# The lead of a gated residual block: how x and c arrive, three unsplit contracted chunks, and half 1's square sum on VectorE

## The chip, the cores and the metric

The kernel runs on one core of a Trainium2 chip. The metric is the device time of one execution in microseconds (us). Five engines share the work: TensorE (PE, with PEld for its weight loads), VectorE (DVE), ScalarE (ACT), GpSimd (POOL) and SyncE (SP), which only issues DMAs.

## The reference

One layer of a streaming encoder, with 1024 positions, 1024 channels and a feed-forward width of 2816, all in fp32:

```
mod = silu(c) @ w_ada + b_ada;  sh1, sc1, g1, sh2, sc2, g2 = split(mod, 6)
h = rms_norm(x, norm_mix_g) * (1 + sc1) + sh1
b, c_s, v, v_c, gl, gates = split(h @ w_in)                  # 7 blocks of 1024 columns
y_a = (b * causal_dwconv3(c_s * v)) @ w_short_out
u = causal_dwconv31(v_c * sigmoid(gl)) + conv_conf_b
y_b = silu(layer_norm(u)) @ w_conf_out
x = x + g1 * ((sigmoid(g_a) * y_a + sigmoid(g_b) * y_b) @ w_o)
h2 = rms_norm(x, norm_ffn_g) * (1 + sc2) + sh2
a, bg = split(h2 @ w_ffn_in);  x = x + g2 * ((silu(a) * bg) @ w_ffn_out)
out = rms_norm(x, final_norm_g)
```

Here `rms_norm` divides by the root of the mean square over the 1024 channels. The host transposes, reorders and packs the inputs.

## The kernel before, in words

Channels lie on partitions: x is held transposed, as eight chunks (k = 0 to 7) of 128 channels by 1024 positions. Positions come in two halves of 512 (h = 0 and 1), as a PSUM bank holds 512 fp32 numbers a partition. A tile of 128x512 is the unit of most steps.

A large matrix product is made of *split* operands. Each operand is cut into a high part in fp32r (a ScalarE copy, `wh` for weights) and a low part, the rest (a subtraction, `wl`). `mm3` (L274) makes a product of three matmuls: high by high (L277), weight high by activation low (L278) and weight low by activation high (L280). The norm sums (`ss` at L393, later `mu` and `var`) are single matmuls of unsplit fp32 operands with a matrix of ones, which also spreads the sum over all partitions.

The **lead** is the first stage. It makes seven blocks of 128 output columns of the input projection (three pairs for the GLU, one gate), contracted over all eight chunks, first for half 0, then for half 1. `row_blocks` (L358) runs chunk by chunk: for each k it makes the operands and then feeds seven accumulating banks; the last two chunks are done together, bank by bank. The operands of chunk k come out of `act_x` (L430):

- two blocks of `w_ada` are loaded and reduced with silu(c) on VectorE (`modulation`, L254, one instruction of 128x1024 at L262 and a short one that reads the sum out). They give scale and shift of the chunk; `affine` (L267) joins the scale to the norm's gain.
- `modulate` (L342) multiplies x by the scale column and the reciprocal root r in one VectorE instruction (L344), ScalarE adds the shift into the high part `h..h` (L346), VectorE makes the low part `h..l` (L347), and ScalarE writes the whole, unsplit h back over x (L350), for sums that later products need.
- `lead_w` (L427) loads and splits the chunk's 128x896 weights: the high part on ScalarE (L203), the low part on VectorE, or on GpSimd for chunks 5 to 7 (L204).

Ahead of that, `squares_x` (L377) loads half 0's x as eight tiles of 128x512, whose rows are 2 KB, squares them on ScalarE (L383) and adds them on VectorE (L388). `norm_start` (L391) sums over partitions on TensorE and starts the reciprocal root on ScalarE (L327), `rstd_end` finishes it in three VectorE steps (L332 to L334). c is loaded spread over 128 partitions (512 KB, L422) and put through Silu in one 128x1024 instruction (L424); the vectors `vec` follow on the same queue (L423). Half 1's x is loaded and squared after chunk 2 (`X1_AT = 2`), and its squares are added on GpSimd (L388); its norm sum and root stand among chunks 4 and 5.

The order is written by hand in places: `tc.issue_after` puts an instruction behind another one on its engine, and `plan` with `next_w` fetches weights two blocks ahead. Nearly all loads go through SP's queue in program order, and one of them waits there, with all behind it, until its buffer is free. Buffers bear on this: `raw` has five (loaded weights), `wh` and `wl` have three each, `uc` has eight (ada blocks in the lead, later the GLU's results and more), PSUM has six banks for `ps` and two for `ps2`.

Behind the lead come one block of gate b, the remaining input columns in pairs (`product`, a seven-product scheme in place of eight block products), the convolutions on VectorE, the two output projections, the joined one and the feed-forward part.

Of the kernel before, what the change touches and what calls it, by code (L numbers as in the profile page):

```python
# [47 lines left out]
CK = 31  # L48
# [12 lines left out]
ADA_ORDER = [b for k in range(KC) for b in (8 + k, k)] + list(range(16, 48))  # L61


LEAD = 7


X1_AT = 2


AHEAD = 2  # L70
# [28 lines left out]
PIECES = [(0, 512), (512, 256), (768, 256)]  # L99


FILL = 264


@with_exitstack
def block_kernel(ctx: ExitStack, tc: tile.TileContext, xT, c, vecs, ada, w_first, w_plain, w_duals,
                 w_short, w_conf, w_o, w_fi, w_fo, w_last, outT):
# [14 lines left out]
    cp = pool("const", 1)  # L122
# [53 lines left out]
    def modc(i):  # L176
        return mod[:, i : i + 1]
# [16 lines left out]
    def weights(src, n=1024, after=(), lo_engine=nc.vector):  # L194
        return split_w(load(src, n), n, after, lo_engine)
# [37 lines left out]
        return {m: (lambda m=m: unit(m)) for m in PRODUCTS}  # L233


    plan = [(w_first[k], LEAD * P) for k in range(KC)]
    plan += [(w_plain[0], 1024)]
    for d in range(len(PAIRS) // 2):
        units = dual_units([w_duals[d, m] for m in range(4)], 1024, eng=nc.gpsimd)
# [5 lines left out]
    def next_w(ahead=AHEAD):  # L245

        fetch(ahead + 1)
        return ready.pop(0)
# [23 lines left out]

    def mm3(outs, wsl, w, xs, first, last, again=False):

        wh, wl = w[0][:, wsl], w[1][:, wsl]
        for ps, (xh, xl) in zip(outs, xs):
            nc.tensor.matmul(ps, wh, xh, start=first, stop=False, skip_group_check=again)  # L277
            nc.tensor.matmul(ps, wh, xl, start=False, stop=False, skip_group_check=again)  # L278
        for ps, (xh, _) in zip(outs, xs):
            mm3.ins = nc.tensor.matmul(ps, wl, xh, start=False, stop=last, skip_group_check=again).ins  # L280
# [61 lines left out]
    def modulate(src, r, scale, shift, name):  # L342

        begin = nc.vector.scalar_tensor_tensor(out=src, in0=src, scalar=scale, in1=r, op0=ALU.mult, op1=ALU.mult)  # L344
        hi, lo = hl_tile(name + "h"), hl_tile(name + "l")
        act = nc.scalar.activation(hi, src, AF.Identity, bias=shift)  # L346
        last = nc.vector.scalar_tensor_tensor(  # L347
            out=lo, in0=src, scalar=shift, in1=f32(hi), op0=ALU.add, op1=ALU.subtract
        )
# [5 lines left out]

        return [(next_w(), act(k)) for k in range(n)]

    def row_blocks(act, n, name, ops=(), unit=lambda k: next_w()):  # L358

        outs = [(ps_tile if o < 6 else ps2_tile)(f"{name}{o}") for o in range(n)]  # L360
        ops = list(ops)
        for k in range(KC):
            if k == len(ops):
                xs = act(k)
                ops.append((unit(k), xs))
            if k == KC - 2:
                continue
            for o in range(n):
                for kk in range(KC - 2, KC) if k == KC - 1 else (k,):
                    w, xs = ops[kk]  # L370
                    mm3([outs[o]], slice(o * P, o * P + P), w, [xs], kk == 0, kk == KC - 1)
        return outs


    x = {}

    def squares_x(h):  # L377

        for k in range(KC):
            x[k, h] = s_tile(f"x{k}{h}")  # L380
            nc.sync.dma_start(x[k, h], xT[k, :, halves[h]])
            sq = g_tile("sq")
            nc.scalar.activation(sq, x[k, h], AF.Square, scale=1.0 / 32.0)  # L383
            if k == 0:
                acc = sq
            else:
                eng = nc.gpsimd if h else nc.vector
                eng.tensor_tensor(acc, acc, sq, ALU.add)  # L388
        return acc

    def norm_start(acc, name, n=H, tile_of=g_tile, ss_tile=ps_tile):  # L391
        ss = ss_tile("ss")
        nc.tensor.matmul(ss[:, :n], ones, acc, start=True, stop=True)  # L393
        return rstd_start(ss, eps1, name, n, tile_of)
# [5 lines left out]
    def uc_tile(name, n=T + CK - 1, dt=F32):  # L400
        return ucp.tile([P, T + CK - 1], dt, tag="uc", name=name)[:, :n]
# [16 lines left out]
        nc.scalar.dma_start(gate_dram[b, j][:, halves[h]], sig)  # L418

    hT = [[None, None] for _ in range(KC)]  # L420
    rx_0 = rstd_end(*norm_start(squares_x(0), "rx0"))
    nc.sync.dma_start(cs, c.to_broadcast([P, D]))  # L422
    nc.sync.dma_start(vec, vecs)  # L423
    silu = nc.scalar.activation(cs, cs, AF.Silu)  # L424
    load_rsqrt(silu.ins)

    def lead_w(k):  # L427
        return weights(w_first[k], LEAD * P, modulate.ins[:1], nc.gpsimd if k > X1_AT + 2 else nc.vector)

    def act_x(k, h):  # L430
        nonlocal rx_1
        if h == 0:
            with ExitStack() as after:
                if k:
                    after.enter_context(tc.issue_after(modulate.ins[0]))
# [3 lines left out]
        hT[k][h] = modulate(x[k, h], rx_1 if h else rx_0, aff1[:, k : k + 1], modc(k), f"h{k}{h}")  # L439
        if h == 0:  # L440
            if k == X1_AT:
                rx_1 = squares_x(1)
            elif k == X1_AT + 2:
                with tc.issue_after(mm3.ins), tc.issue_after(modulate.ins[1]):
                    rx_1 = norm_start(rx_1, "rx1", ss_tile=ps2_tile)
            elif k == X1_AT + 3:
                with tc.issue_after(modulate.ins[2]):
                    rx_1 = rstd_end(*rx_1)
        return hT[k][h]

    rx_1 = None
    for h in range(2):
        lead = row_blocks(lambda k: act_x(k, h), LEAD, "lead", **({} if h else {"unit": lead_w}))
        for j in range(LEAD // 2):
            glu(j, h, lead[2 * j], lead[2 * j + 1])
        gate("b", 0, h, lead[-1])
# [124 lines left out]


    taps = vec[:, V_CW : V_CW + CK // 2 * 2 * KC].rearrange("p (j two k) -> p j two k", two=2, k=KC)
    nc.vector.tensor_tensor(wsum.rearrange("p (j k) -> p j k", k=KC), taps[:, :, 0], taps[:, :, 1], ALU.add)
# [369 lines left out]
    n = 2 * GROUP * P  # L954
# [77 lines left out]
    for i in range(len(PIECES)):  # L1032
        acc, sqs = sqs[0] if i else None, []
# [85 lines left out]
```

## Time and profile before

| | us |
|---|---|
| median of 3 runs | 1529.91 (1529.85 to 1535.77) |
| the profiled execution | 1529.94 |
| its span, first to last instruction | 1528.0 |
| TensorE busy | 1468.8 (96%) |
| VectorE busy | 1183.9 (77%) |
| ScalarE busy | 616.9 (40%) |
| GpSimd busy | 597.2 (39%) |
| mean granted TensorE clock | 0.989 |
| first lead matmul; first of half 1 | 20.34; 73.02 |

A matmul's duration in the profile includes its way through the array, so that following ones overlap; the cost in a stream is the distance of their starts. An unsplit fp32 matmul shows as two records. A group's idle time is that of its engine just before it, with the engine or DMA that ended it. The execution took 1.9 us more than its span; that lies around the program.

### The profile page before, as it was taken

The page shows a single profiled execution, that of the slowest core. Times are in us where ns is not written, and L with a number is a line of the kernel's source. Part 1 is how long each engine was busy: PE and PEld are TensorE (multiplying, and loading weights), DVE is VectorE, ACT ScalarE, POOL GpSimd, SP SyncE. Part 2 cuts the span into 40 slices and gives each one's busy share as a digit, 9 for nine tenths or more (in the row PEclk, how much of TensorE's full clock was granted, in tenths as well). Part 3 has the DMA queues.
Part 4 walks back from the last instruction along what each step waited for, and adds up shares of the span by engine and source line. Part 5 has one row for each costly group of instructions (what it writes and reads, how often), then busy time and mean ns, then how long its engine had stood idle before and what let it go on. Part 6 is the DMA issues. An engine that isn't in the chain of part 4 may idle for free.

```text
span 1528.0 us, 17853 instructions
## 1 busy us (share of the span) xinstructions
PE 1468.8 (96%) x6466; PEld 1205.1 (79%) x6466; DVE 1183.9 (77%) x1559; ACT 616.9 (40%) x873; POOL 597.2 (39%) x493
## 2 busy tenths in 40 slices
PE   5799999999998999999999989999999999999996
PEld 3688887877886888878788868888888888888886
DVE  7987898999998882757876798877766765677756
ACT  5563433333333343325334464444444443221234
POOL 1326788798768884310121101110000016535005
PEclk9999999999999999999999999999999999999998
DMA  9432214223222249755665527644444449999403
GB/s 363 161 101 69 97 56 152 69 97 111 97 69 97 70 171 393 262 182 178 236 203 158 173 83 234 207 152 155 153 153 152 154 150 367 351 304 274 129 15 111
DMA packets 88024, 256.16 MB, mean 168 GB/s; under 512 B 10112, under 2 KB 12288, under 8 KB 87936
## 3 DMA queue, kind: packets, MB, share of 16 engines
q1 hardware_dynamic: 47248, 147.01, 29.0%
q0 software_dynamic: 36944, 95.44, 19.2%
q10 hardware_dynamic: 3744, 12.58, 2.0%
q8 instruction: 50, 0.82, 0.2%
q14 instruction: 38, 0.31, 0.1%
HBM read 188.41 MB, written 66.58 MB: 167 GB/s over the span
## 4 chain that ended last, share of the span: by engine, by line
PE 67%; DVE 15%; DMA 6%; POOL 5%; issue 5%; ACT 1%; SPq 0%; DVEq 0%; ACTq 0%; POOLq 0%
PE x L280 10%; PE x L278 9%; PE x L277 9%; DVE c L604 6%; PE z L278 5%; PE z L280 5%; PE z L277 5%; PE y L277 3%; PE y L278 3%; PE y L280 3%; POOL wl L204 3%; DMA raw<-in_ada 2%; PE mix L277 2%; PE mix L278 2%; PE mix L280 2%
## 5 line engine op out<-in xcount | busy, mean ns | idle before, releaser
L203 ACT CAST wh<-raw 128x1024 fp32r<-128x1024 f32 (+2 forms) x260 | 262.0, 1009 | 406.1 <-PE z L278 100.6
L204 POOL TENSOR_TENSOR wl<-raw,wh 128x1024 fp32r<-128x1024 f32 (+1 forms) x95 | 243.1, 2564 | 96.3 <-ACT wh L203 89.8
L204 DVE TENSOR_TENSOR wl<-raw,wh 128x1024 fp32r<-128x1024 f32 (+2 forms) x165 | 190.2, 1155 | 50.4 <-ACT wh L203 47.8
L604 DVE SCALAR_TENSOR_TENSOR c<-diff,vec,c 128x512 f32<-128x512 f32 x248 | 182.5, 750 | 3.7
L867 POOL DMA_DIRECT2D hid<-stage x71 | 37.8, 533 | 356.2 <-DVE stage L317 350.8
L277 PE MATMUL x<-th,wh 128*128 128x512 f32 x336 | 130.7, 389 | 0.0
L278 PE MATMUL x<-tl,wh 128*128 128x512 f32 x336 | 130.7, 389 | 0.0
L280 PE MATMUL x<-th,wl 128*128 128x512 f32 x336 | 130.7, 389 | 0.0
L604 DVE SCALAR_TENSOR_TENSOR c<-u,wsum,c 128x512 f32<-128x512 f32 x112 | 84.2, 752 | 2.0
L277 PE MATMUL x<-t2h,wh 128*128 128x512 f32 x184 | 73.8, 403 | 5.5 <-ACT wh L203 2.8
L280 PE MATMUL x<-t2h,wl 128*128 128x512 f32 x184 | 73.5, 400 | 5.2 <-POOL wl L204 4.9
L278 PE MATMUL x<-t2l,wh 128*128 128x512 f32 x184 | 73.6, 400 | 0.1
L262 DVE CUSTOM_DVE_ANT_0 raw<-raw,cs,vec 128x1024 f32<-128x1024 f32 x24 | 33.7, 1405 | 51.6 <-DMA raw<-in_ada 47.6
L278 PEld LDWEIGHTS x<-tl,wh 128*128 128x128 f32 x336 | 63.1, 188 | 13.2
L280 PEld LDWEIGHTS x<-th,wl 128*128 128x128 f32 x336 | 63.1, 188 | 13.1
L277 PEld LDWEIGHTS x<-th,wh 128*128 128x128 f32 x336 | 63.1, 188 | 13.0
L280 PE MATMUL z<-th,wl 128*128 128x512 f32 x168 | 65.5, 390 | 0.0
L277 PE MATMUL z<-th,wh 128*128 128x512 f32 x168 | 65.4, 389 | 0.0
L278 PE MATMUL z<-tl,wh 128*128 128x512 f32 x168 | 65.4, 389 | 0.0
L316 ACT CAST stage<-g 128x512 fp32r<-128x512 f32 x62 | 38.3, 620 | 52.0 <-DVE g L856 24.7
L893 POOL DMA_DIRECT2D th<-hid x71 | 37.9, 534 | 52.0 <-PE x L280 31.8
L317 DVE TENSOR_TENSOR stage<-g,stage 128x512 fp32r<-128x512 f32 x62 | 42.5, 688 | 17.2 <-ACT stage L316 16.9
(811 smaller groups left out, 4091.0 us busy)
## 6 DMA issues: line engine op xcount, KB each, us to landing
hid<-stage POOLq DMA_DIRECT2D x71, 512.0 KB, 4.2
raw<-in_w_fi SPq DMA_DIRECT2D x50, 512.0 KB, 4.1
raw<-in_w_duals SPq DMA_DIRECT2D x48, 512.0 KB, 3.6
th<-hid POOLq DMA_DIRECT2D x71, 256.0 KB, 5.8
tl<-hid POOLq DMA_DIRECT2D x71, 256.0 KB, 5.9
ada<-in_ada SPq DMA_DIRECT2D x24, 512.0 KB, 7.7
raw<-in_ada SPq DMA_DIRECT2D x24, 512.0 KB, 4.7
raw<-in_w_fo SPq DMA_DIRECT2D x24, 384.0 KB, 5.9
```

The costliest lines, as they stand in the source:

```text
L203: nc.scalar.copy(wh, raw)
L204: lo = lo_engine.tensor_tensor(wl, raw, f32(wh), ALU.subtract)
L262: nc.vector.tensor_tensor_reduce(out=raw, in0=raw, in1=cs, scale=1.0, scalar=col(V_ADA, b), op0=ALU.mult, op1=ALU.add, accum_out=modc(b),)
L277: nc.tensor.matmul(ps, wh, xh, start=first, stop=False, skip_group_check=again)
L278: nc.tensor.matmul(ps, wh, xl, start=False, stop=False, skip_group_check=again)
L280: mm3.ins = nc.tensor.matmul(ps, wl, xh, start=False, stop=last, skip_group_check=again).ins
L316: nc.scalar.copy(hi, src)
L317: nc.vector.tensor_tensor(lo, src, f32(hi), ALU.subtract)
L604: tap.ins = nc.vector.scalar_tensor_tensor(out=out, in0=src[:, s : s + H], scalar=wt, in1=acc, op0=ALU.mult, op1=ALU.add).ins
L867: nc.gpsimd.dma_start(hid_dram[key], s)
L893: nc.gpsimd.dma_start(t, hid_dram[key][:, s])
```

## The change

It rebuilds the lead; all behind it keeps its code, but for `wsum`, a small sum of convolution weights, which moves behind a modulate.

- Half 0's x comes from a second array `x0`, in which two chunks lie side by side: four loads of 128x1024 with rows of 4 KB. They take four of the eight `uc` buffers; `modulate` reads them and writes into a new tile.
- c is loaded as one row on ScalarE's queue, and so is `vec`. Two fp32 matmuls with a row of ones spread c over the partitions in PSUM, where Silu reads it in two instructions of 128x512, behind the squares. A one-column Silu at the start loads its table.
- For half 0's chunks 0 to 2 (`WHOLE = 3`) neither weights nor h are split: `mm3` makes one fp32 matmul of the loaded weights and the whole h. Their h is split in half 1, and all weights are loaded again there, as before.
- Half 0's last two chunks are no longer joined (`joined=1`). All low parts of weights in the lead are made on VectorE.
- Half 1's x is loaded after chunk 5 (`X1_AT = 5`), squared and added on VectorE in chunk 6, its norm sum stands in chunk 6, the root's end behind chunk 7. Half 1's first operands are made ahead of half 0's GLUs.
- `FILL`, a tile that only shifts addresses, grows by 32 bytes a partition, and there is one more small constant tile.

```diff
+WHOLE = 3
-X1_AT = 2
+X1_AT = 5
-FILL = 264
+FILL = 272
...
     def mm3(outs, wsl, w, xs, first, last, again=False):
+        if w[1] is None:
+            for ps, x in zip(outs, xs):
+                mm3.ins = nc.tensor.matmul(ps, w[0][:, wsl], x, start=first, stop=last).ins
+            return
...
-    def modulate(src, r, scale, shift, name):
-        begin = nc.vector.scalar_tensor_tensor(out=src, in0=src, scalar=scale, in1=r, op0=ALU.mult, op1=ALU.mult)
+    def modulate(src, r, scale, shift, name, begun=None):
+        begin = nc.vector.scalar_tensor_tensor(
+            out=src, in0=src if begun is None else begun, scalar=scale, in1=r, op0=ALU.mult, op1=ALU.mult
+        )
+        if name is None:
+            act = nc.scalar.activation(src, src, AF.Identity, bias=shift)
+            modulate.ins = begin.ins, act.ins, begin.ins
+            return None
...
-    def squares_x(h):
-        for k in range(KC):
-            x[k, h] = s_tile(f"x{k}{h}")
-            nc.sync.dma_start(x[k, h], xT[k, :, halves[h]])
+    def squares_x(src, acc=None):
+        for t in src:
             sq = g_tile("sq")
...
-                eng = nc.gpsimd if h else nc.vector
-                eng.tensor_tensor(acc, acc, sq, ALU.add)
+                add = nc.vector.tensor_tensor(acc, acc, sq, ALU.add)
...
-    rx_0 = rstd_end(*norm_start(squares_x(0), "rx0"))
-    nc.sync.dma_start(cs, c.to_broadcast([P, D]))
-    nc.sync.dma_start(vec, vecs)
-    silu = nc.scalar.activation(cs, cs, AF.Silu)
+    crow = diffp.tile([P, T + CK - 1], F32, tag="diff", name="diff")[:1, :D]
+    nc.scalar.dma_start(crow, c)
+    nc.scalar.dma_start(vec, vecs)
+    nc.scalar.activation(cp.tile([P, 1], F32, name="si"), ones[:, :1], AF.Silu)
+    xin = {}
+    for k in range(0, KC, 2):
+        t = uc_tile("x0", T)
+        nc.sync.dma_start(t, x0[k // 2])
+        xin[k], xin[k + 1] = (t[:, s] for s in halves)
+    cb = []
+    for s in halves:
+        cb.append(ps_tile("cb"))
+        nc.tensor.matmul(cb[-1], ones[:1], crow[:, s], start=True, stop=True)
+    acc = squares_x([xin[k] for k in range(KC)])
+    with tc.issue_after(squares_x.ins[0]):
+        for s, t in zip(halves, cb):
+            silu = nc.scalar.activation(cs[:, s], t, AF.Silu)
     load_rsqrt(silu.ins)
+    rx_0 = rstd_end(*norm_start(acc, "rx0"))
     def lead_w(k):
-        return weights(w_first[k], LEAD * P, modulate.ins[:1], nc.gpsimd if k > X1_AT + 2 else nc.vector)
+        if k < WHOLE:
+            return load(w_first[k], LEAD * P), None
+        return weights(w_first[k], LEAD * P, modulate.ins[:1])
...
             if k == X1_AT:
-                rx_1 = squares_x(1)
-            elif k == X1_AT + 2:
+                for i in range(KC):
+                    x[i, 1] = s_tile(f"x{i}1")
+                    nc.sync.dma_start(x[i, 1], xT[i, :, halves[1]])
+            elif k == X1_AT + 1:
+                with tc.issue_after(modulate.ins[2]):
+                    rx_1 = squares_x([x[i, 1] for i in range(KC)])
                 with tc.issue_after(mm3.ins), tc.issue_after(modulate.ins[1]):
                     rx_1 = norm_start(rx_1, "rx1", ss_tile=ps2_tile)
-            elif k == X1_AT + 3:
+            elif k == KC - 1:
                 with tc.issue_after(modulate.ins[2]):
                     rx_1 = rstd_end(*rx_1)
+            if whole:
+                return x[k, 0]
+        elif k < WHOLE:
+            hT[k][0] = split(x[k, 0], hl_tile, f"h{k}0")
         return hT[k][h]
...
+    ops = ()
     for h in range(2):
-        lead = row_blocks(lambda k: act_x(k, h), LEAD, "lead", **({} if h else {"unit": lead_w}))
+        lead = row_blocks(lambda k: act_x(k, h), LEAD, "lead", ops, **({} if h else {"unit": lead_w, "joined": 1}))
+        if h == 0:
+            xs = act_x(0, 1)
+            ops = [(next_w(), xs)]
...
+        "x0": x[:H].T.reshape(KC // 2, 2, P, H).transpose(0, 2, 1, 3).reshape(KC // 2, P, T),
```

More of the change, by code (lines that the diff above doesn't have):

```diff
@@ L99, with block_kernel @@
 PIECES = [(0, 512), (512, 256), (768, 256)]
-FILL = 264
+FILL = 272
 @with_exitstack
-def block_kernel(ctx: ExitStack, tc: tile.TileContext, xT, c, vecs, ada, w_first, w_plain, w_duals,
+def block_kernel(ctx: ExitStack, tc: tile.TileContext, x0, xT, c, vecs, ada, w_first, w_plain, w_duals,
                  w_short, w_conf, w_o, w_fi, w_fo, w_last, outT):
@@ L233, in dual_units @@
         return {m: (lambda m=m: unit(m)) for m in PRODUCTS}
-    plan = [(w_first[k], LEAD * P) for k in range(KC)]
+    plan = [None] * KC
     plan += [(w_plain[0], 1024)]
@@ L356, in first_operands, with row_blocks @@
         return [(next_w(), act(k)) for k in range(n)]
-    def row_blocks(act, n, name, ops=(), unit=lambda k: next_w()):
+    def row_blocks(act, n, name, ops=(), unit=lambda k: next_w(), joined=2):
         outs = [(ps_tile if o < 6 else ps2_tile)(f"{name}{o}") for o in range(n)]
@@ L365, in row_blocks @@
                 ops.append((unit(k), xs))
-            if k == KC - 2:
+            if KC - joined <= k < KC - 1:
                 continue
             for o in range(n):
-                for kk in range(KC - 2, KC) if k == KC - 1 else (k,):
+                for kk in range(KC - joined, KC) if k == KC - 1 else (k,):
                     w, xs = ops[kk]
@@ L375, in block_kernel @@
     x = {}
-    def squares_x(h):
-        for k in range(KC):
-            x[k, h] = s_tile(f"x{k}{h}")
-            nc.sync.dma_start(x[k, h], xT[k, :, halves[h]])
+    def squares_x(src, acc=None):
+        for t in src:
             sq = g_tile("sq")
-            nc.scalar.activation(sq, x[k, h], AF.Square, scale=1.0 / 32.0)
-            if k == 0:
+            act = nc.scalar.activation(sq, t, AF.Square, scale=1.0 / 32.0)
+            if acc is None:
                 acc = sq
             else:
-                eng = nc.gpsimd if h else nc.vector
-                eng.tensor_tensor(acc, acc, sq, ALU.add)
+                add = nc.vector.tensor_tensor(acc, acc, sq, ALU.add)
+        squares_x.ins = act.ins, add.ins
         return acc
@@ L433, in act_x @@
             with ExitStack() as after:
-                if k:
-                    after.enter_context(tc.issue_after(modulate.ins[0]))
+                after.enter_context(tc.issue_after(modulate.ins[0] if k else squares_x.ins[1]))
                 for i in range(2 * k, 2 * k + 2):
@@ L438, in act_x @@
             affine(aff1, k, 8, V_GMIX)
-        hT[k][h] = modulate(x[k, h], rx_1 if h else rx_0, aff1[:, k : k + 1], modc(k), f"h{k}{h}")
+            x[k, 0] = s_tile(f"x{k}0")
+        whole = h == 0 and k < WHOLE
+        hT[k][h] = modulate(x[k, h], rx_1 if h else rx_0, aff1[:, k : k + 1], modc(k),
+                            None if whole else f"h{k}{h}", None if h else xin[k])
         if h == 0:
             if k == X1_AT:
-                rx_1 = squares_x(1)
-            elif k == X1_AT + 2:
+                for i in range(KC):
[4 more added lines that the diff above has]
+                    rx_1 = squares_x([x[i, 1] for i in range(KC)])
                 with tc.issue_after(mm3.ins), tc.issue_after(modulate.ins[1]):
                     rx_1 = norm_start(rx_1, "rx1", ss_tile=ps2_tile)
-            elif k == X1_AT + 3:
+            elif k == KC - 1:
                 with tc.issue_after(modulate.ins[2]):
                     rx_1 = rstd_end(*rx_1)
+            if whole:
+                return x[k, 0]
+        elif k < WHOLE:
+            hT[k][0] = split(x[k, 0], hl_tile, f"h{k}0")
         return hT[k][h]
     rx_1 = None
+    plan[:KC] = [lambda k=k: weights(w_first[k], LEAD * P, [modulate.ins[2 if k else 0]]) for k in range(KC)]
+    ops = ()
     for h in range(2):
-        lead = row_blocks(lambda k: act_x(k, h), LEAD, "lead", **({} if h else {"unit": lead_w}))
+        lead = row_blocks(lambda k: act_x(k, h), LEAD, "lead", ops, **({} if h else {"unit": lead_w, "joined": 1}))
+        if h == 0:
+            xs = act_x(0, 1)
+            ops = [(next_w(), xs)]
         for j in range(LEAD // 2):
@@ L583, in block_kernel @@
     taps = vec[:, V_CW : V_CW + CK // 2 * 2 * KC].rearrange("p (j two k) -> p j two k", two=2, k=KC)
-    nc.vector.tensor_tensor(wsum.rearrange("p (j k) -> p j k", k=KC), taps[:, :, 0], taps[:, :, 1], ALU.add)
+    with tc.issue_after(modulate.ins[0]):
+        nc.vector.tensor_tensor(wsum.rearrange("p (j k) -> p j k", k=KC), taps[:, :, 0], taps[:, :, 1], ALU.add)
     cv_dram = [dram.tile([P, T], F32, name=f"cv{j}") for j in range(KC)]
```

## The prediction

> **What bounds the kernel now.** I first cut the span into stretches. Columns: stretch, its length, then busy time (and count) of PE, PEld, DVE, ACT and POOL, the granted clock, DMA share, GB/s.
>
> ```profile
> 0.00:75.00 75.00, 47.90 (x181) 36.28 (x182) 64.68 (x93) 40.36 (x57) 18.95 (x15) 0.95 0.72 265
> 75.00:125.00 50.00, 50.00 (x222) 41.40 (x222) 43.67 (x53) 30.00 (x46) 16.38 (x8) 1.00 0.27 80
> 125.00:600.00 475.00, 466.24 (x2039) 382.69 (x2038) 409.02 (x527) 179.66 (x244) 374.89 (x164) 1.00 0.33 114
> ```
>
> TensorE is idle for 27 of the first 75 us, never in the next 50 and for 9 of the 475 after that. The lead is the only place in the first 600 us with much to gain, and what it gains reaches the end: behind it TensorE is the bound. From the end of the lead on (a few instructions later on VectorE and ScalarE) the changed program issues the same instructions in the same order on every engine.
>
> Then TensorE's waits up to 75 us (total, count, longest) and its time line.
>
> ```profile
> PE ss L393 <- DVE sq L388: 12.2, 1, 12.2
> PE lead L277 <- ACT h00h L346: 6.0, 1, 6.0
> PE lead L278 <- DVE h30l L347: 4.7, 1, 4.7
> PE lead L277 <- ACT h60h L346: 1.9, 1, 1.9
> PE lead L277 <- ACT h70h L346: 1.4, 1, 1.4
> PE lead L277 <- ACT h30h L346: 0.8, 1, 0.8
> ```
> ```profile
> 20.34 1.22 PE L277 MATMUL lead<-h00h,wh 128*128 128x512 f32 x2 [6.02 <-ACT h00h L346]
> ...
> 43.45 0.80 PE L278 MATMUL lead<-h30l,wh 128*128 128x512 f32 x1 [4.69 <-DVE h30l L347]
> ...
> 73.02 0.39 PE L277 MATMUL lead<-h01h,wh 128*128 128x512 f32 x1
> ```
>
> Call the first lead product P0 (20.34 now) and the first product of half 1 T1 (73.02 now). Split products stand 0.227 us apart, so half 0's 168 and one norm sum (0.87, below) need 39 of those 52.7 us. The 13.7 lost are 8.8 of waits (4.7, 1.9, 1.4, 0.8) and about 5 of products 0.43 apart, behind 20.34 and again behind 43.45: half rate after TensorE stood still. The long wait is for h30l, and the time line of VectorE and GpSimd shows why it is late:
>
> ```profile
> 37.95 3.98 POOL L388 TENSOR_TENSOR sq<-sq 128x512 f32<-128x512 f32 x2 [0.30 <-ACT sq L383]
> ```
> ```profile
> 36.45 2.16 DVE L204 TENSOR_TENSOR wl<-raw,wh 128x896 fp32r<-128x896 f32 x1
> 38.53 2.29 DVE L262 CUSTOM_DVE_ANT_0 ada<-ada,cs,vec 128x1024 f32<-128x1024 f32 x1
> ```
>
> These two take 1.08 and 1.28 where GpSimd is idle. Half 1's adds on GpSimd slow VectorE, and half 1's x (2 MB) stands ahead of chunk 4's loads.
>
> **The change, part by part.**
>
> *Start.* Let L be when the last of half 0's x lands. It is 10.2 now: issued at 4.0, 6.2 to landing. The stretches of the queue:
>
> ```profile
> 2.00:8.00 6.00, 0.00 (x0) 0.00 (x0) 1.39 (x2) 2.26 (x5) 0.00 (x0) 1.00 0.96 289
> 8.00:10.00 2.00, 0.00 (x0) 0.00 (x0) 1.48 (x3) 1.85 (x4) 0.00 (x0) 1.00 1.02 352
> 10.00:20.00 10.00, 2.07 (x2) 0.50 (x2) 8.10 (x14) 6.73 (x9) 0.00 (x0) 1.00 1.02 408
> 27.00:33.00 6.00, 6.00 (x29) 4.95 (x28) 5.96 (x11) 4.18 (x7) 0.06 (x1) 1.00 1.06 392
> ```
>
> By 10.2 some 2.6 MB have moved, of which 2.1 are x and 0.5 belong to transfers still under way. After the change 0.19 MB of vec share the engines, issued by ScalarE; c is one row of 4 KB. So 2.8 MB must move. At the rates of now that is done at 10.9; at 408 GB/s, the rate of 4 KB rows from 10 us on, at 2.0 + 6.8 = 8.8. The profile does not tell whether 2 to 8 us are slow because of 2 KB rows or because the program has just started: half 1's 2 KB rows (27 to 33 us) move at 392. I take the middle, 9.7, and keep 8.8 and 10.9 for the range.
>
> From L on: two squares 1.3; two Silus out of PSUM, 1.2 (rows of 0.6 of that shape, overlapping slightly), their table now loaded ahead, and the 0.5 MB load of the spread c gone; then the chain as it stands now: two reductions with a column, 2.6 (21.11 to 23.71), three steps of the reciprocal root 2.2, the scaling 0.8, ScalarE's bias 0.8. With semaphores 9.0. Beside it, and not later: the last add (L+2.05), the norm sum at half rate (2.1), a table load, the root (to L+4.9, when the reductions end at L+5.2). So P0 = 18.7: 1.6 earlier. The two products that spread c (4 x 0.86 at half rate) lie in idle time.
>
> *Half 0 on TensorE.* The price of an unsplit fp32 product is in the two of the mean:
>
> ```profile
> 602.93 0.40 PE L280 MATMUL ya<-q71h,wl 128*128 128x512 f32 x1
> 603.17 1.88 PE L635 MATMUL mu<-tot,ones 128*128 128x512 f32 x4
> ...
> 605.12 0.39 PE L278 MATMUL ya<-q00l,wh 128*128 128x512 f32 x1
> ```
>
> From 603.16 to 604.89 (one step before 605.12) is 1.73 for two products, 0.865 each, against 0.68 for three split ones. Whole chunks cost 21 x 0.185 = 3.9 us more on TensorE. They buy slack: VectorE does 3.3 us a whole chunk (two reductions 2.4, column 0.2, scaling 0.67, as they stand between 21.11 and 24.38) against 4.95 with a weight's low part 1.0 and h's 0.67.
> Sum: chunk 0 with 3.5 us at half rate, as now: 2 x 1.73 + 5 x 0.865 = 7.8; chunks 1 and 2, 12.1; chunks 3 to 7, 105 x 0.227 = 23.8; norm sum 0.87: 44.6.
>
> *Is everything there in time?* Times from P0; VectorE's first reduction starts at -6.4. At 408 GB/s loads land 1.28 us apart for 512 KB and 1.12 for 448 KB, from L on, so a chunk (two blocks of ada, one of weights) every 3.7. Chunk 1 is ready at 3.2 (needed 7.8), 2 at 6.5 (13.9), 3 at 10.7 (19.9), 4 at 15.7 (24.7), 5 at 20.7 (29.4). The added waits: four buffers for ada instead of eight (x holds four), so ada 4 waits for the reduction of ada 0, at -5.2, while 3.5 us of loads are queued: no gap. TensorE now reads raw weights, so the load of chunk 5's weights waits on SP's queue until TensorE ends chunk 0 (7.8), that of chunk 6 until it ends chunk 1 (13.9), and behind that stand half 1's x and the last ada. They land by 17.0, 22.4 and 25.0; chunk 7's weights, behind chunk 2, by 26.1. Chunk 6's cast needs one of three wh buffers, free at 24.7: ready at 29.0 (34.2). Then VectorE adds half 1's squares, 7 x 0.6, between the last pair of reductions: sum at 36.6, wanted at 36.25 inside chunk 6, a stall of 0.35. h70l is there at 38.3 (40.2). Then root 2.2, scaling, a weight low, two scalings, one glu and h01l: 45.1, and TensorE wants it at 45.2. No slack is left there; one bank of half 1 is free 0.2 late. T1 = P0 + 45.0 = 63.7, and with the 0.2 the shift is 9.1 us.
>
> *At nothing.* Three splits of the whole chunks' half 0 (3 x 0.6 on ScalarE and on VectorE) in half 1, where VectorE is idle for 5.7 of 12 us from 100 us on; without that cover 1.8. GpSimd loses all its lead work; nothing waits for it. wsum, the wider fill and an early table load: idle time.
>
> The profiled execution took 1529.94 us (span 1528.0), the median of the runs is 1529.91. **Forecast: 1529.9 - 9.1 = 1520.8.**
>
> **Rivals.**
> *x lands no earlier.* L = 10.9: P0 = 19.9, gain 7.9, 1522.0. For it: 2 KB rows reach 392 of 408 GB/s later in this trace. Against: at 7.65 ScalarE had waited 1.53 us for the fourth of the eight transfers alone; fewer and longer rows leave fewer chances for that. The Trainium skill (DMA: Bandwidth & Descriptors, Specifications) puts full line rate at 512 B and more a piece, which by itself gives this rival; the trace agrees from 27 us on, not before 8.
> *VectorE is late at the border of the halves.* That chain has no slack; were its rows 10% longer from chunk 3 on (36 us), 3.6 us late, 1524.4. For: rows of 2.6 and 3.15 us stand where 0.74 and 1.28 are usual. Against: each lies beside GpSimd's work, which goes. The Trainium skill (TensorE: Matmul & The Clock Gate, Part 1) has the clock fall after about 3.4 us of idling; the trace agrees, with 4 us at half rate behind the 4.7 us wait, and by that rule this wait of 3.6 us could cost 2 more, 1526.4.
> *Slower: TensorE stays at half rate in the unsplit products.* 21 x 1.73 = 36.3 instead of 19.9, and chunk 3 still pays 1.8: 18.2 more, 1539.0. It decides against the change once more than 10 of 21 run so. For: no row shows over 1.7 us of unsplit products in a row, and the one at 12.24 is at half rate. Against: those at 603 us keep 0.43 a pass at full rate.
>
> **How the numbers follow.** Forecast with x landing at 8.8 to 10.2 and at most 1 us of other waits: 0.54, 1519.8 to 1522. x no earlier: 0.16, half of it on either side of 0.5%. VectorE late: 0.22, 1522.5 to 1525.5. Half rate: 0.04. Other stalls past no change: 0.04. Range 1519.0 to 1525.0: below, L = 8.8 with no other wait (1519.9) and a half-rate stretch that costs 0.9 less than its 1.75; above, most of the late border. 0.5% is 7.6 us, about what a measurement of this kernel can tell from no change: faster by more 0.54 + 0.08 = 0.62, within 0.30, slower 0.08.
>
> **What would show it.** Right: first lead product at 17.8 to 19.9; unsplit products 0.865 apart after some 3.5 us; no wait over 1 us between them and half 1; half 1 begins near 63.7; VectorE's rows at 1.08 and 1.28 throughout; from there the old trace, 9 us earlier. Wrong: a wait for h01l or ss of several us, unsplit products at 1.7, x landing after 11, or loads of chunks 5 to 7 ending a wait.

## The result, and the profile after

The changed kernel took **1522.29 us** (median of 5 runs, 1519.83 to 1522.63) where the kernel before, beside it on the same chip, took 1532.41 (median of 5, 1529.85 to 1535.77). The ratio is **0.9929**, with a 95% interval of 0.9910 to 0.9949: faster by about 0.7%. The forecast was 1520.8, range 1519.0 to 1525.0. The profiled execution took 1522.49 (span 1520.7).

The same three stretches, with the same columns (stretch, length, busy time and count of PE, PEld, DVE, ACT, POOL, granted clock, DMA share, GB/s):

```profile
0.00:75.00 75.00, 62.58 (x206) 39.92 (x207) 64.19 (x108) 43.24 (x65) 0.53 (x5) 1.00 0.75 279
75.00:125.00 50.00, 50.00 (x222) 41.42 (x221) 43.92 (x50) 26.82 (x41) 22.42 (x11) 1.00 0.25 75
125.00:600.00 475.00, 465.40 (x2031) 381.25 (x2030) 408.49 (x525) 177.59 (x240) 375.91 (x164) 1.00 0.35 120
```

TensorE is idle for 12.4 of the first 75 us instead of 27.1; GpSimd's 18.95 us there have become 0.53. Behind that TensorE is as busy as before (50.00 of 50 us, then 465.40 of 475 against 466.24). TensorE's waits up to 75 us, and the places in its time line where half 0, the split chunks and half 1 begin:

```profile
PE ss L404 <- DVE sq L398: 5.5, 1, 5.5
PE lead L279 <- ACT x L354: 4.6, 1, 4.6
PE cb L444 <- DMA diff<-in_c: 2.3, 1, 2.3
```
```profile
18.24 20.43 PE L279 MATMUL lead<-x,raw 128*128 128x512 f32 x42 [4.56 <-ACT x L354]
38.11 0.80 PE L283 MATMUL lead<-h30h,wh 128*128 128x512 f32 x1
...
63.46 0.39 PE L283 MATMUL lead<-h01h,wh 128*128 128x512 f32 x1
63.69 0.40 PE L284 MATMUL lead<-h01l,wh 128*128 128x512 f32 x1
```

All three waits lie ahead of the first lead product. The four inside half 0 (4.7, 1.9, 1.4, 0.8) are gone. P0 is 18.24 (20.34 before), and half 1 begins at T1 = 63.46 (73.02). The 21 unsplit products, 42 records, fill 18.24 to 38.11. VectorE at the border of the halves has its usual durations again, and is just in time:

```profile
54.85 1.08 DVE L206 TENSOR_TENSOR wl<-raw,wh 128x896 fp32r<-128x896 f32 x1
...
62.71 0.74 DVE L359 SCALAR_TENSOR_TENSOR h01l<-x,mod,h01h 128x512 fp32r<-128x512 f32 x1
```

h01l is ready at 63.45 and TensorE's first product of it stands at 63.69. The first transfers:

```profile
2.00:8.00 6.00, 3.75 (x4) 1.15 (x4) 1.71 (x3) 3.90 (x7) 0.00 (x0) 1.00 0.94 365
8.00:10.00 2.00, 0.00 (x0) 0.00 (x0) 1.75 (x3) 1.78 (x4) 0.00 (x0) 1.00 1.02 416
```

They were 289 and 352 GB/s. The last x of half 0 lands at L = 8.86 (10.25 before). This moves from execution to execution: it is 8.53 to 8.87 in the ten profiles of kernels with this start, and 9.63 in a second profile with the start of before (e4), whose P0 is 0.6 earlier.

### The profile page after: what moved, and what is told of

It is laid out like the page before. It is cut to its first block, busy times and chain, and to the rows that moved or that the text cites. A ratio compares the mean times of both kernels' runs of the same rounds, so it can differ in the third digit from the quotient of the medians.

```text
span 1520.7 us, 17802 instructions
## 1 busy us (share of the span) xinstructions
PE 1474.4 (97%) x6449; PEld 1202.4 (79%) x6449; DVE 1179.8 (78%) x1566; ACT 612.5 (40%) x871; POOL 580.9 (38%) x483
## 4 chain that ended last, share of the span: by engine, by line
PE 77%; DVE 10%; DMA 5%; POOL 3%; issue 3%; ACT 1%; SPq 0%; DVEq 0%; ACTq 0%; POOLq 0%
PE x L286 11%; PE x L283 11%; PE x L284 11%; PE z L283 6%; PE z L286 6%; PE z L284 6%; PE y L284 4%; PE y L283 4%; PE y L286 4%; DVE c L647 3%; DMA raw<-in_ada 2%; PE mix L283 2%; PE mix L284 2%; PE mix L286 2%; PE yb L284 2%
## 5 line engine op out<-in xcount | busy, mean ns | idle before, releaser
L206 POOL TENSOR_TENSOR wl<-raw,wh 128x1024 fp32r<-128x1024 f32 x92 | 237.2, 2586 | 85.5 <-ACT wh L205 85.3
L228 POOL TENSOR_TENSOR raw<-raw 128x1024 f32<-128x1024 f32 x12 | 29.2, 2436 | 98.6 <-DVE wl L206 94.0
L322 ACT CAST stage<-g 128x512 fp32r<-128x512 f32 x62 | 38.3, 621 | 55.7 <-DMA hid<-stage 27.8
```

The lines of the kernel that those rows point to most:

```text
L206: lo = lo_engine.tensor_tensor(wl, raw, f32(wh), ALU.subtract)
L228: eng.tensor_tensor(a["s1"], a["21"], a["22"], ALU.add)
```

## The experiments

T1 turned out to be a poor mark, since in some kernels the first products of half 1 run ahead and then wait. I use the first product of chunk 3 of half 1 (h31h) as well, T3: by then every kernel is in step. It lies at 87.30 before and at 77.87 after, 9.4 us earlier. All times are of one profiled execution each, ratios are against the kernel before on the same chip, "rest" is the span behind T3.

| kernel | P0 | T1 | T3 | rest | ratio, 95% interval |
|---|---|---|---|---|---|
| before | 20.34 | 73.02 | 87.30 | 1440.7 | 1 |
| after | 18.24 | 63.46 | 77.87 | 1442.8 | 0.9929 (0.9910 to 0.9949) |
| e1 after, all chunks split | 18.14 | 66.35 | 84.12 | 1440.5 | 0.9964 (0.9951 to 0.9977) |
| e2 after, rows of 2 KB | 18.73 | 64.62 | 78.90 | 1440.4 | 0.9939 (0.9921 to 0.9957) |
| e3 after, adds on GpSimd | 18.16 | 68.21 | 82.49 | 1439.6 | 0.9968 (0.9957 to 0.9978) |
| e4 before, adds on VectorE | 19.72 | 69.07 | 83.35 | 1441.3 | 0.9983 (0.9974 to 0.9993) |
| e5 after again | 18.11 | 63.72 | 78.11 | 1438.7 | 0.9928 (0.9909 to 0.9946) |
| e6 after, c spread by its load | 19.98 | 64.45 | 78.88 | 1442.1 | 0.9940 (0.9921 to 0.9960) |
| e7 after, early place | 18.03 | 62.66 | 76.94 | 1438.5 | 0.9923 (0.9901 to 0.9945) |
| e8 after, kept warm | 19.10 | 61.97 | 79.04 | 1439.6 | 0.9933 (0.9915 to 0.9951) |
| e9 new start alone | 18.16 | 72.35 | 86.63 | 1440.9 | 0.9994 (0.9982 to 1.0006) |
| e10 early place, adds on GpSimd | 18.23 | 63.04 | 78.78 | 1438.9 | 0.9927 (0.9912 to 0.9942) |
| e11 early place, two unsplit | 17.97 | 61.52 | 78.20 | 1440.1 | 0.9925 (0.9912 to 0.9939) |
| e12 early place, warm | 18.14 | 61.03 | 77.59 | 1442.5 | 0.9916 (0.9901 to 0.9931) |

**e1, all chunks split.**
```diff
-WHOLE = 3
+WHOLE = 0
```


> The changed kernel with WHOLE = 0: all eight chunks of half 0 are split into high and low parts. TensorE does 21 x 0.185 = 3.9 us less, VectorE three low parts of weights (1.0 each) and three of h (0.67 each) more, 5 us. Theory A (the whole chunks are worth their price because VectorE sets the pace of half 0): the chain on VectorE at the border of the halves comes 5 us later than the 45.2 of the changed kernel, so half 1 starts 49 to 51 us behind the first lead product, with waits for h or ss before it, and the time is 3.5 to 5.5 us longer. Rival B (TensorE sets the pace and the split was never needed): half 1 starts 41 to 42 us behind the first lead product and the time is some 3.9 us shorter.

Chunk 3 begins 3.1 us sooner (35.02), as TensorE's cheaper products promise, and then it is all lost: T3 is 6.3 us later, the time 5.4 us longer by the two ratios. TensorE's waits behind P0:

```profile
PE lead L283 <- ACT h01h L358: 2.6, 1, 2.6
PE lead L283 <- ACT h70h L358: 1.9, 1, 1.9
PE lead L283 <- ACT h11h L358: 1.4, 1, 1.4
```

Half 1 started 48.2 us behind P0, slightly sooner than theory A's 49 to 51, and waited inside it instead. A holds, B falls: the split products are cheaper on TensorE and dearer in all.

**e2, rows of 2 KB.**
```diff
-        nc.sync.dma_start(t, x0[k // 2])
+        for s in halves:
+            nc.sync.dma_start(t[:, s], x0[k // 2][:, s])
```


> The changed kernel with each of the four tiles of half 0's x loaded by two transfers of rows of 2 KB instead of one of 4 KB; the bytes and the tiles are the same. If short rows are what made the first 8 us slow in the kernel before, the last x lands at 10.0 to 10.5 instead of 8.86 and the first lead product comes 1.1 to 1.6 us later (19.4 to 19.8, time +1.3). If row size does nothing here and the gain came from what else shared the engines, the last x lands at 8.7 to 9.2 and nothing moves by over 0.4 us.

L is 9.91, 1.05 later, so rows of 2 KB do cost time in the first 10 us. The edit also makes eight transfers of four, each half as large; the two were not taken apart. P0 moves by 0.49 only: with pieces that land singly, the squares and their adds lie less far behind the last one (P0 = L + 8.8 instead of L + 9.4).

**e3, the adds on GpSimd at their late place.**
```diff
-                add = nc.vector.tensor_tensor(acc, acc, sq, ALU.add)
+                add = eng.tensor_tensor(acc, acc, sq, ALU.add)
```
with eng = nc.gpsimd for half 1.

> The changed kernel with the seven adds of half 1's square sum on GpSimd again, at their late place. Theory A (GpSimd's adds slow VectorE, and they take some 2 us each themselves): the sum comes 8 to 10 us later, VectorE's rows beside it stand at 2 us and more, TensorE waits for the norm sum; half 1 starts 51 to 56 us behind the first lead product instead of 45.2 and the time is 6 to 10 us longer. Rival C (the place matters, the engine does not): within 1.5 us of the changed kernel.

TensorE waits for the sum, 50.05 us behind P0 half 1 begins, T3 is 4.6 us later, the time 6.0 us longer by the two ratios. The row, and VectorE's beside GpSimd:

```profile
56.10 1.12 PE L404 MATMUL ss<-sq,ones 128*128 128x512 f32 x2 [2.90 <-POOL sq L398]
```
```profile
52.63 2.29 DVE L264 CUSTOM_DVE_ANT_0 ada<-ada,cs,vec 128x1024 f32<-128x1024 f32 x1
...
54.86 2.14 DVE L206 TENSOR_TENSOR wl<-raw,wh 128x896 fp32r<-128x896 f32 x1
```

Theory A in kind, with a smaller size than I gave it. C falls.

**e4, one part alone on the kernel before.**
```diff
-                eng = nc.gpsimd if h else nc.vector
+                eng = nc.vector
```


> The kernel before with one part alone: the seven adds of half 1's square sum on VectorE, at their early place (behind chunk 2). VectorE gains 7 x 0.69 = 4.8 us of work and loses the stretching of its rows beside GpSimd, about 9.5 us by the rows from 33 to 60 us (1.25, 1.86, 2.16, 2.29, 1.09, 2.06, 2.60 and 1.42 against 0.16, 0.75, 1.08, 1.28, 0.16, 1.08, 0.75 and 0.16). Theory A (several parts share the gain): half 1 starts at 68 to 71 instead of 73.0, time -2 to -5 us. Rival D (GpSimd alone is the whole story): half 1 starts before 66, time -7 us or more. Rival E (x of half 1 ahead of chunk 4's loads is the whole story): no gain, 72.5 or later.

T1 is 69.07 and the time 2.6 us shorter: the parts share the gain. Of the 4.0 us at T3, 0.6 are there at P0 already, ahead of any of these adds. The wait for h30l shrinks from 4.7 to 0.7, and others take its place in the chunks behind, those below and one of 1.6 for the sum itself:

```profile
PE lead L277 <- ACT h60h L346: 1.8, 1, 1.8
PE lead L277 <- ACT h50h L346: 1.7, 1, 1.7
PE lead L277 <- ACT h70h L346: 1.4, 1, 1.4
PE lead L278 <- DVE h30l L347: 0.7, 1, 0.7
```

**e5, the same kernel again.** No edit.

> The changed kernel once more. In its first profile TensorE waits 1.55 us at 1309.12 (the reload of x1[4] lands late), a wait that none of the profiles of the first four experiments shows, though they have the same program there. If that wait is chance of one execution, this profile is without it and stands at a span of 1518 to 1519.5 with half 1 beginning at 63.2 to 63.8; if it belongs to the changed start, it is here again and the span is 1520 to 1521.

This is about the one thing in the first profile of after that I could not place: the row where the lead over the kernel before falls from 8.8 to 7.1 us (first TensorE, then VectorE).

```profile
1309.12 0.47 PE L283 MATMUL z<-th,wh 128*128 128x512 f32 x1 [1.55 <-ACT wh L205]
```
```profile
1308.27 0.75 DVE L991 SCALAR_TENSOR_TENSOR x<-z,ng,x 128x512 f32<-128x512 f32 x1 [6.66 <-DMA x<-x_dram]
```

The row names a cast that had ended at 1308.20. What ends just ahead of 1309.12 is VectorE's row (at 1309.02), which empties a bank and had waited for a reload of x1 on GpSimd's queue; I take that as what TensorE waited for. In e5 the wait at this place is 0.39, the span 1516.8 (below my 1518 to 1519.5). A wait of over 1 us stands there in 3 of the 14 profiles (after, e6 and e12). It is chance of one execution and not part of the change.

**e6, c spread by its load.**
```diff
-    nc.scalar.dma_start(crow, c)
+    nc.scalar.dma_start(cs, c.to_broadcast([P, D]))
...
-        for s, t in zip(halves, cb):
-            silu = nc.scalar.activation(cs[:, s], t, AF.Silu)
+        silu = nc.scalar.activation(cs, cs, AF.Silu)
```


> The changed kernel with c spread over the 128 partitions by its load (0.5 MB, first on ScalarE's queue) and one Silu over 1024 elements from SBUF, without the two products that spread it. Theory A (bytes ahead of x cost their time at the rate of about 400 KB per us): the last x lands at 9.9 to 10.3 instead of 8.86, the first lead product comes 0.5 to 1.3 us later (18.7 to 19.5), and half 1 begins as much later. Rival (the spread by TensorE buys nothing, the load hides beside x): the last x lands at 8.7 to 9.2, the first lead product at 18.0 to 18.5.

L is 10.54 and P0 19.98: the 0.5 MB cost 1.7 us there, more than the 1.25 at 400 KB per us. T3 moves by 1.0 only, since TensorE's half rate behind P0 was shorter in this execution (2.7 us instead of 4.4).

**e7, the early place.**
```diff
-X1_AT = 5
+X1_AT = 2
...
                     rx_1 = squares_x([x[i, 1] for i in range(KC)])
+            elif k == X1_AT + 2:
                 with tc.issue_after(mm3.ins), tc.issue_after(modulate.ins[1]):
```


> The changed kernel with half 1's x loaded behind chunk 2 instead of chunk 5, its squares with chunk 3 and its norm sum with chunk 4 (as early as in the kernel before), adds on VectorE, three unsplit chunks. Theory A (the place alone is worth little, once the adds are off GpSimd and the unsplit chunks have given VectorE a lead): half 1 begins 45 to 46.5 us behind the first lead product, as in the changed kernel (45.2). Rival (2 MB ahead of chunk 4's loads is what cost the kernel before its time): 48 us or more behind it, with waits for h30, h40 or h50.

Half 1 begins 44.6 us behind P0, 0.6 sooner than in the changed kernel and 0.4 below theory A's range, with no wait inside half 0. The place of half 1's x is worth nothing by itself once the unsplit chunks are there.

**e8, TensorE kept busy ahead of P0.**
```diff
+    for _ in range(4):
+        nc.tensor.matmul(cb[-1], ones, acc, start=True, stop=True)
```
between the norm sum and the last steps of its root.

> The changed kernel with four more products of ones and the square sum into a bank that nobody reads, behind the norm sum, while TensorE waits for the first scaled x (it waits 4.56 us there). If the half rate of the first five unsplit products (0.86 us a pass-pair of 0.43) comes from TensorE's having stood still, the first lead products now stand 0.43 apart in the records and the three unsplit chunks take 17.9 to 18.6 us instead of 19.87; half 1 begins at 61.5 to 63.3, less than that gain, since the chain on VectorE at the border has little slack. If the half rate is bound to the program's start or to the first unsplit products themselves, they stay at 0.86 and nothing moves.

```profile
11.67 2.08 PE L404 MATMUL ss<-sq,ones 128*128 128x512 f32 x2 [4.79 <-DVE sq L398]
13.54 5.72 PE L452 MATMUL cb<-sq,ones 128*128 128x512 f32 x8
19.10 18.19 PE L279 MATMUL lead<-x,raw 128*128 128x512 f32 x42
36.72 0.80 PE L283 MATMUL lead<-h30h,wh 128*128 128x512 f32 x1
```

The first lead products are 0.43 apart, the three chunks take 17.6 us, and chunk 3 begins 1.4 us sooner although P0 is 0.86 late. It buys nothing: in half 1's first chunk TensorE waits 0.6 us for VectorE and 1.4 for h11h, and T3 is 1.2 us later. The four products also changed the order that the scheduler chose from chunk 6 on: the norm sum stands later, and ScalarE has h11h behind a cast that itself waits for a buffer of TensorE's. That loss is not the border chain on VectorE that I had named, or not it alone.

**e9, the new start alone.**
```diff
-WHOLE = 3
+WHOLE = 0
-X1_AT = 5
+X1_AT = 2
...
-        return weights(w_first[k], LEAD * P, modulate.ins[:1])
+        return weights(w_first[k], LEAD * P, modulate.ins[:1], nc.gpsimd if k > X1_AT + 2 else nc.vector)
...
-                    rx_1 = squares_x([x[i, 1] for i in range(KC)])
+                    rx_1 = squares_x([x[i, 1] for i in range(KC)], eng=nc.gpsimd)
+            elif k == X1_AT + 2:
...
-            elif k == KC - 1:
+            elif k == X1_AT + 3:
```


> The new start alone: x in rows of 4 KB, c spread by TensorE and the early table load as in the changed kernel, but half 1's x early (behind chunk 2), its adds on GpSimd, the low parts of the weights of chunks 5 to 7 on GpSimd, and all chunks split, as in the kernel before. Theory A (the parts add up): the first lead product at 18.0 to 18.4, half 1 some 51.5 to 53.5 us behind it, so at 69.5 to 71.8 and a time 1.2 to 3 us shorter than before. Rival (the earlier start is given back while TensorE waits for h30l behind GpSimd's adds): half 1 at 72.5 or later, no gain.

The run keeps more of the changed kernel than its name says: half 0's last two chunks stay apart, half 1's first operands stay ahead of the GLUs, and half 1's squares stand one chunk later than before. The rival holds in its outcome. P0 is 2.2 us earlier and T1 0.7 us, and the time is that of the kernel before (0.9994). The wait is not the one that the rival named; TensorE's largest is now for the sum from GpSimd:

```profile
36.14 1.43 PE L283 MATMUL lead<-h30h,wh 128*128 128x512 f32 x5 [1.06 <-ACT h30h L358]
...
45.63 2.07 PE L404 MATMUL ss<-sq,ones 128*128 128x512 f32 x2 [4.41 <-POOL sq L398]
...
49.07 0.80 PE L284 MATMUL lead<-h40l,wh 128*128 128x512 f32 x1 [0.94 <-DVE h40l L359]
```

**e10, early place with the adds on GpSimd and three unsplit chunks.** The edit of e7 and that of e3 together.

> The changed kernel with half 1's x early and the seven adds on GpSimd, three unsplit chunks: against the run with the early place alone, only the engine of the adds differs. Theory A (GpSimd's adds cost wherever they stand): some seven of VectorE's rows from 29 to 45 us take 1 us more, seven adds of 0.69 less, and the sum itself is ready at 44 to 46 instead of 38; TensorE waits for it or for h40, and half 1 begins 46.5 to 49 us behind the first lead product (44.6 with the adds on VectorE). Rival (the lead of the unsplit chunks covers it in this place): 44 to 45.5.

44.8 us behind P0: the rival again by T1 and by the time (0.9927 against 0.9923 in e7). By T3, the better mark, the adds on GpSimd still cost 1.8 us: in half 1's first chunk TensorE waits several times, up to 0.3 us, for VectorE to empty a bank. Here GpSimd's adds slow VectorE as in e3, but VectorE had been standing still:

```profile
30.09 0.75 DVE L359 SCALAR_TENSOR_TENSOR h30l<-x,mod,h30h 128x512 fp32r<-128x512 f32 x1 [2.87 <-ACT h30h L358]
33.50 2.12 DVE L206 TENSOR_TENSOR wl<-raw,wh 128x896 fp32r<-128x896 f32 x1 [2.65 <-ACT wh L205]
35.55 2.29 DVE L264 CUSTOM_DVE_ANT_0 ada<-ada,cs,vec 128x1024 f32<-128x1024 f32 x1
...
37.77 2.30 DVE L264 CUSTOM_DVE_ANT_0 ada<-ada,cs,vec 128x1024 f32<-128x1024 f32 x1
```

Three rows are 3.1 us longer together, and 5.5 us of idle time stand ahead of them. Read against e9: the unsplit chunks, with the low parts of the weights of chunks 5 to 7 on VectorE and the root at chunk 7, bring T3 forward by 7.9 us and the ratio from 0.9994 to 0.9927. These three were not taken apart, and half 1's x is also asked for 5.4 us sooner (20.23 against 25.65).

**e11, two unsplit chunks at the early place.** The edit of e7, and WHOLE = 2.

> The run with the early place with two unsplit chunks instead of three: TensorE 7 x 0.185 = 1.3 us less, VectorE one low part of a weight and one of h more, 1.75. In that run VectorE stands still for 2.85 us ahead of h30l. Theory A (that idle time takes the 1.75 in): half 1 begins 43.2 to 44.0 us behind the first lead product instead of 44.6, time 0.5 to 1.4 us shorter. Rival (every unsplit chunk is needed for the border of the halves): 45.5 or more, with a wait for h01.

Half 1 begins 43.55 us behind P0 as theory A has it, and then waits 1.4 for h11h, as in e8; T3 is 1.3 later than in e7, the time the same (0.9925). Two chunks or three make no difference that shows.

**e12, early place with three products to keep TensorE busy.** The edit of e7 and that of e8, with range(3).

> The run with the early place with three more products of ones and the square sum behind the norm sum (four of them ended 0.9 us after the first scaled x was there and delayed the first lead product by that). Theory A: TensorE's half rate ends some 6 us after the norm sum began, by 18, so the unsplit chunks take 17.6 to 18.3 us; at the border of the halves the chain on VectorE has 0.85 us of slack in that run, so half 1 begins at 61.4 to 62.2 instead of 62.66 and no more is gained. Rival (VectorE's slack there is not what limits): 61.2 or earlier without any wait behind it, time 1.4 to 2 us shorter.

The unsplit chunks take 17.7 us without a product at half rate. T1 is 61.03, since four products of h01h run ahead of h01l, and the gain is given back in the next chunk: T3 (77.59) is 0.65 later than in e7. ScalarE's rows there, and TensorE's wait:

```profile
66.31 0.94 ACT L205 CAST wh<-raw 128x896 fp32r<-128x896 f32 x1 [2.26 <-PE lead L284]
67.16 0.72 ACT L358 ACTIVATE h11h<-x,mod 128x512 fp32r<-128x512 f32 x1
```
```profile
67.93 1.66 PE L283 MATMUL lead<-h11h,wh 128*128 128x512 f32 x6 [1.43 <-ACT h11h L358]
```

The cast of a coming chunk's weights waits for a buffer that TensorE frees, and h11h, for which TensorE waits next, stands behind it on ScalarE. So theory A was right that no more is gained, and these rows point to another limit than the one it named: an order on ScalarE. This is argued and not shown, as an order with h11h ahead of that cast was not tried. VectorE has a part in it too: it scales the x of h11h only from 65.3 to 66.0, where the changed kernel has done so by 62.2. By these rows an estimate is that some 1.1 of the 1.43 us hang on the cast. The ratio, 0.9916, is the lowest of all, but the value of the changed kernel (0.9929) lies inside its interval: no version was shown to be faster.

## Why the prediction was right, and where it was not

**The total.** 1520.8 against a median of 1522.29, and 1520.88 (median of 4) in e5. The shift at T1, 9.1 forecast, is 9.56. Side by side the medians differ by 10.1 us and the ratio gives 10.9 (7.8 to 13.8), since the kernel before took 1532.41 there and not the 1529.9 of the forecast. The 1.5 us between forecast and median are no step of the sum: the rest behind T3 ran from 1438.5 to 1442.8 in fourteen profiles whose kernels do the same work there, and the two of the changed kernel stand at 1442.8 and 1438.7.

**The start: two errors of opposite sign.** The middle value L = 9.7 was wrong and the lower bound right: 8.86. Both causes between which the profile could not tell are real. Up to 3.2 us the start is slow with either row (from 1.4 to 3.2 us 220 GB/s before, 228 in e2, 171 after). From 3.2 to 8 us the rows tell: 286 before, 308 in e2, 399 after, and e2 lands 1.05 later. c's spread load was no part of that choice, as it stood behind x; ahead of x it would have cost 1.7 (e6). The page cited for the rival that x lands no earlier (the Trainium skill, DMA: Bandwidth & Descriptors, Specifications) has full line rate from 512 B on; e2 speaks against that for the first 10 us, where the same bytes in 2 KB rows, and in twice as many transfers, land 1.05 us later. From L to P0 I had 9.0, it is 9.38. The step that failed is "the last add (L+2.05)". The adds hang on each other and stand 0.80 apart, not 0.69:

```profile
6.88 4.67 DVE L398 TENSOR_TENSOR sq<-sq 128x512 f32<-128x512 f32 x6 [0.46 <-ACT sq L394]
11.47 1.28 DVE L264 CUSTOM_DVE_ANT_0 ada<-ada,cs,vec 128x1024 f32<-128x1024 f32 x1
...
14.44 0.69 DVE L338 SCALAR_TENSOR_TENSOR rx0t<-rx0r 128x512 f32<-128x512 f32 x1 [0.41 <-ACT rx0r L333]
```

Six adds in a row from 6.88 on end at 11.55, L + 2.7, and the root is 0.41 later than the reductions that I had named as the later ones. P0 came out 0.46 better than forecast.

**Half 0.** The 21 unsplit products: 19.9 forecast, 19.87 measured. The stretch at half rate was 4.4 us, not 3.5, and the products at full rate 0.855, not 0.865; that the two cancel is luck. The stall for the sum was put at 0.35 and was at most 0.1, since the scheduler put the norm sum behind the products of three of chunk 6's seven outputs. The border was to be met at 45.1 against 45.2; it was met with 0.24 to spare. From chunk 6 on the chain on VectorE came as forecast, in us from P0: h60l at 29.0 (29.0), the sum at 36.7 (36.6), h70l at 38.4 (38.3), h01l at 45.2 (45.1).

**The reason.** Here the text was half right. It named two causes of the 13.7 us lost before, GpSimd's adds and half 1's x ahead of chunk 4's loads, and the unsplit chunks as slack that is bought for 3.9 us. The slack is nearly the whole of it. In order of T3: the start alone gives 0.7 (e9), the unsplit chunks with what went with them 7.9 more (e10), the adds on VectorE 1.8 (e7), the late place minus 0.9 (after). Put first on the kernel before, the adds on VectorE are worth 4.0 (e4), or 3.3 from P0 on. Two profiles with one start differ by 0.6 at P0 (before and e4), so the 0.7 and the 0.9 are not clear of chance. The two durations that decide stood in the prediction side by side and were not set against each other there: a split chunk takes 21 x 0.227 = 4.77 on TensorE and 4.95 on VectorE. VectorE could not get ahead, so what came on top of it (an add, a stretched row, a late load) reached TensorE. An unsplit chunk takes 6.06 and 3.3, and leaves 2.8 each. The traces show this lead. In the changed kernel VectorE has finished h30l 8.9 us before TensorE's first product of it:

```profile
29.08 0.75 DVE L359 SCALAR_TENSOR_TENSOR h30l<-x,mod,h30h 128x512 fp32r<-128x512 f32 x1
```
```profile
38.74 0.40 PE L284 MATMUL lead<-h30l,wh 128*128 128x512 f32 x1
```

In e1 the same distance is 1.1 (34.10 and 35.24), in the kernel before 0.05. In e7 and e10 it is 7.5; loads and adds take most of that by chunk 4 (2.5 and 1.3 are left), and TensorE waits for nothing inside half 0. With this lead the place of x no longer matters (e7) and the adds on GpSimd cost 1.8 by T3 and nothing that the ratio shows (e10); without it even the changed order loses 6.3 (e1). At the late place GpSimd's adds cost 4.6 again (e3), though the lead is not used up there: h60l is ready 9.9 us ahead, and TensorE waits 2.9 us for GpSimd's sum itself and then runs at half rate.

**The rivals.** x no earlier: no, L is 1.4 earlier. VectorE late at the border: no, 0.24 us early. What is next there is the wait for h11h: e8, e11 and e12 took 1.1 to 1.6 us off half 0 and lost it there. Half rate in all unsplit products: no, 0.43 a pass from the sixth on.

**At nothing.** The three splits moved into half 1, wsum and the wider fill: no wait of TensorE from P0 to 75 us in the changed kernel, so this held.

## What to carry to other kernels

Where one engine prepares operands for another, set the two durations of one step against each other before pricing any single disturbance: if the feeder is slower by even 4% (4.95 against 4.77 here), it has nothing in hand for a disturbance, and work moved from the feeder to the bound engine can pay although the bound engine gets more to do. An earlier start is worth only what the first wait behind it leaves of it (2.2 us became 0.7). And a gain ahead of a place without slack (e8, e11, e12) moves the wait and not the end: look at what the next operand is queued behind.

## What the runs showed of the hardware

- **Half rate that the granted clock does not show.** Behind P0, after 4.56 us of waiting, the records of unsplit products stood 0.85 apart for 2.7 to 6.1 us (e6 2.7, e10 3.5, e7 3.6, e11 4.2, after 4.4, e3 5.1, e5 5.2, e2 6.1) while the column of the granted clock read 1.00. In e12 TensorE was busy without a break from 11.52 on; there the half rate lasted until 17.65, and no lead product ran at it. The records ahead of P0 (cb and ss) stand 0.85 apart too, so these runs do not tell whether the wait or the program's start brings the half rate about. The Trainium skill (TensorE: Matmul & The Clock Gate, Part 1) lets the clock go up after a busy window of about 3.4 us that runs on its own, not from the first product; that the lengths differ from run to run agrees with that, but their spread, 2.7 to 6.1, is wider than the 500 ns either way that the page gives, and 6.1 is longer than one window.
- **The same wait with and without it.** At 478 to 488 us TensorE waits for a low part of weights from GpSimd in every profile, 1.2 to 3.5 us. Half rate followed all five waits of 3.46 to 3.49 us, five of the seven of 2.52 to 2.56, and neither of the two of 1.24 and 1.32. Behind the 3.48 us of after the granted clock of the next stretch is 0.62; behind the 2.54 of e5 it is 1.00:

```profile
479.00:483.50 4.50, 4.45 (x12) 3.50 (x13) 4.50 (x8) 0.50 (x1) 4.50 (x2) 0.62 0.63 151
```
```profile
478.00:481.50 3.50, 3.06 (x13) 2.55 (x14) 3.50 (x6) 0.47 (x1) 3.50 (x3) 1.00 0.61 172
```

  The half rate is 1.6 us of the 4.1 between the rests of the two profiles of one kernel, the longer wait ahead of it 0.9, and the wait at 1309 us another 1.2.
- **What stays open.** By the ratios most of the kernels with unsplit chunks gain some 1 to 3 us more than their T3 tells (after 10.9 against 9.4, e12 12.9 against 9.7), with intervals of 2 to 3 us on either side. A part of it is that T3 is measured against one execution of the kernel before, of 1529.94, whose medians beside the others are 1529.94 to 1532.41. Whether the remainder is more than the spread of the rest was not settled.
